# Layer-0 attention: 512-column evictions of the probabilities, V's two parts multiplied onto the same rows for later queries, and output casts on GpSimd

## The chip, the cores and the metric

The kernel runs on one core of a Trainium2 chip. The metric is the device time of one execution in microseconds (us), the median of several runs. Five engines matter: TensorE (PE; its weight loads are shown as PEld), VectorE (DVE), ScalarE (ACT), GpSimd (POOL) and SyncE (SP), which issues most DMAs. Each works through its own queue in order, and waits on semaphores for the others.

## The reference

The model is a trunk of four layers over 512 latent tokens and 256 context tokens, width 1024. Each layer has a mixer (grouped attention, neighbourhood attention, a convolution module, a Fourier mixer) and a squared-ReLU MLP. Only the mixer of layer 0 concerns the change: attention with 16 query heads, 4 key and value heads, and a head width of 64. Latent queries look at all 768 keys, context queries at the 256 context keys alone.

```
def gqa_attend(q, k, v):
    s = jnp.einsum('bqkgd,bnkd->bkgqn', q, k, preferred_element_type=jnp.float32)
    p = jax.nn.softmax(s, axis=-1).astype(v.dtype)
    return jnp.einsum('bkgqn,bnkd->bqkgd', p, v)
...
k_all = jnp.concatenate([kc, kl], axis=1)
yl = gqa_attend(q_latent, k_all, v_all) @ w_o      # in blocks of 128 queries
yc = gqa_attend(q_context, kc, vc) @ w_o
```

Everything is float32. The kernel's matmuls take operands of type float32r, and it splits a float32 operand in two such parts: H, the value cast to float32r, and L, what is left (the value minus H). A product of two split operands is then H*H + H*L + L*H, and sometimes L*L as well.

## The kernel before, in words

The stage of the change is `l0b`. It works on 8 pairs of heads. Each pair has three parts of 256 queries: part 0 (latent queries 0 to 255), part 1 (latent queries 256 to 511) and part 2 (the context queries). Parts 0 and 1 have 6 chunks of 128 keys, part 2 has 2. A work item is one head (`hh`) of one part of one pair, 48 in all. For each item `front` is called twice, for `u` = 0 and 1, 128 queries each, and `back` is called twice, one item behind: its first half stands between the two fronts of the next item, its second half after them.

`front` multiplies the scores on PE into a PSUM tile `s` (L612; two such tiles), takes the negated maximum of each row on DVE (L614), and the exponential with the row's sum on ACT (L616). It then transposes the probabilities on PE, three chunks of 128 x 128 to one PSUM tile `st` (L621; three such tiles), and evicts each of these tiles with `split` (L104, L105): ACT casts it to the tile H of the transposed probabilities (`pt[0]`), and DVE subtracts to get L (`pt[1]`). In part 2 a front has only two chunks.

`back` multiplies V by these probabilities (L635). `vp` holds for each key chunk and each key head 128 columns, 64 of V's H and then 64 of V's L, so one matmul with 128 weight columns gives H's product in PSUM rows 0 to 63 and L's in rows 64 to 127. It is done once with `pt[0]` and once with `pt[1]`; 256 columns (both query halves) stream through. There is one PSUM tile `pv`; the two heads of a pair take 256 columns each. When the second head is complete, `recip_rows` makes the reciprocals of the sums (DVE, L555), spreads each over 64 columns (DVE, L557), transposes that on PE (L559) and copies it out on ACT (L561) as `rb`. `fold` adds PSUM rows 64 to 127 to rows 0 to 63, or the other way round for the second head: an ACT copy (L567) and a DVE add (L568) for each head. `scale_pv` multiplies by `rb` on POOL (L573), casts to H on ACT (L104) and subtracts for L on POOL (L105).

A planner inside the framework sets the order of instructions on each engine, from the order in which the program issues them and from its own estimate of durations; the order is then fixed. Instructions that are issued earlier go first where both are ready. Two instructions on different engines that touch one PSUM tile follow each other.

Towards the end of the stage the first weights of the output projection are loaded and split (ACT casts, POOL or DVE subtracts, 1024 columns each). The projection starts on PE as soon as the attention's last matmuls are issued, and takes the eight pairs' outputs in order, the context queries in its second half. `recip_rows` is also called by layer 1's attention.

Of the kernel before, what the change touches and what calls it, by code (L numbers as in the profile page):

```python
# [9 lines left out]
F = mybir.dt.float32  # L10
R = mybir.dt.float32r
BF = mybir.dt.bfloat16
AF = mybir.ActivationFunctionType
ALU = mybir.AluOpType
AX = mybir.AxisListType

P = 128
# [7 lines left out]
HD = 64  # L25
# [24 lines left out]
class Trunk:  # L50
# [496 lines left out]
                            nc.tensor.transpose(pt[:, i * P:(i + 1) * P], pf[s][:, t, 2 * hp + hh].rearrange("p s d -> p (s d)"), self.ident)  # L547
                    nc.scalar.copy(out=self.kd[:, 2 * hp:2 * hp + 2, s, c0:c0 + 256], in_=pt.rearrange("p (h t) -> p h t", h=2))

    def recip_rows(self, sums, w, wk, rp):  # L550

        nc = self.nc
        nb = w // P
        rs = wk.tile([P, nb, 2], F, tag="rs", name="rs", bufs=3)
        nc.vector.reciprocal(out=rs, in_=sums)  # L555
        re = self.tmp("q", w)
        nc.vector.tensor_copy(out=re.rearrange("p (b h d) -> p b h d", b=nb, h=2), in_=rs.unsqueeze(3).to_broadcast([P, nb, 2, HD]))  # L557
        for b in range(nb):
            nc.tensor.transpose(rp[:, b * P:(b + 1) * P], re[:, b * P:(b + 1) * P], self.ident)  # L559
        rb = self.tmp("r", w)  # L560
        nc.scalar.copy(out=rb, in_=rp[:, :w])  # L561
        return rb
# [13 lines left out]
    def l0b(self):  # L576
        nc, io = self.nc, self.io
        self.psum("psum4", s=(2, 2))
        op = self.open("o0", "right")
        o = [op.tile([P, 2, TALL], R, name=f"o0_{j}") for j in range(KC)]  # L580
        wk = self.open("att0", "right")
        qs, groups, heads, pvs = {}, {}, {}, {}

        def load(pair):
            qs[pair] = self.kv.tile([P, 2, TALL], R, tag="q", name="q", bufs=2)
# [3 lines left out]
        def keys(part):  # L589
            return (0, 6) if part < 2 else (4, 2)  # L590

        def alloc(pair, part, hh):
            n = len(heads)
            pool, bufs = (self.pools["att0b"], 1) if n % 3 == 2 and "att0b" in self.pools else (wk, 2)
            heads[pair, part, hh] = [pool.tile([P, 2, 6, P], R, tag=f"pt{s}", name=f"pt{s}", bufs=bufs)[:, :, :keys(part)[1]] for s in range(2)]

        def front(pair, part, hh, u):

            k0, nk = keys(part)
            if hh == u == 0:  # L600
                groups[pair, part] = wk.tile([P, 2, 2], F, tag="sums", name="sums", bufs=3)
            if u == 0 and (pair, part, hh) not in heads:
                alloc(pair, part, hh)
            q, sums, pt = qs[pair], groups[pair, part], heads[pair, part, hh]
            ps = self.ps("s")
            t0 = part * 256 + u * P
            kc = k0 * P
            for c0, c1 in ((0, 512), (512, TALL)):
                if c1 <= kc:
                    continue  # L610
                for s in range(2):
                    nc.tensor.matmul(ps[:, c0:c1], q[:, hh, t0:t0 + P], self.kd[:, pair // 2, s, c0:c1], start=(s == 0), stop=(s == 1))  # L612
            mx = self.small(1, "m")
            nc.vector.tensor_reduce(out=mx, in_=ps[:, kc:TALL], axis=AX.X, op=ALU.max, negate=True)  # L614
            p = wk.tile([P, TALL], F, tag="p", name="p", bufs=3)
            nc.scalar.activation(p[:, kc:], ps[:, kc:TALL], AF.Exp, bias=mx, accum_out=sums[:, u, hh:hh + 1])  # L616
            for c in range(k0, 6, 3):
                n = min(3, 6 - c)
                pp = self.ps("st")
                for i in range(n):  # L620
                    nc.tensor.transpose(pp[:, i * P:(i + 1) * P], p[:, (c + i) * P:(c + i + 1) * P], self.ident)  # L621
                pw = pp[:, :n * P].rearrange("p (c q) -> p c q", c=n)
                self.split(pw, pt[0][:, u, c - k0:c - k0 + n], pt[1][:, u, c - k0:c - k0 + n])

        def back(pair, part, hh, half):

            k0, nk = keys(part)
            if hh == half == 0:
                pvs[pair, part] = self.ps("pv")
            sums, pv = groups[pair, part], pvs[pair, part]  # L630
            pt = heads[pair, part, hh]
            o_ = pv[:, hh * 256:hh * 256 + 256]
            for c in range(k0 + half * nk // 2, k0 + (half + 1) * nk // 2):
                for s in range(2):
                    nc.tensor.matmul(o_, self.vp[:, c, pair // 2].rearrange("p s d -> p (s d)"), pt[s][:, :, c - k0],  # L635
                                     start=(hh == s == 0 and c == k0), stop=(hh == s == 1 and c == 5))
            if hh == half == 1:
                t0 = part * 256
                rb = self.recip_rows(sums, 256, wk, self.ps("st"))
                t = self.tmp("t", 256)  # L640
                for e in range(2):
                    self.fold(pv[:, e * 256:e * 256 + 256], e, t)
                self.scale_pv(t, rb, (o[pair][:, 0, t0:t0 + 256], o[pair][:, 1, t0:t0 + 256]))

        work = [(pair, part, hh) for pair in range(8) for part in range(3) for hh in range(2)]
        alloc(0, 0, 0)
        load(0)
        for i in range(len(work) + 1):
# [709 lines left out]
```

## Time and profile before

| | |
|---|---|
| median of 3 runs | 2746.52 us (2746.07 to 2748.45) |
| profiled execution | 2748.76 us, its span 2747.0 us |
| granted clock of PE, mean | 0.985 of 2.4 GHz |
| PE busy | 2638.0 us, 96% of the span |
| DVE busy | 1776.1 us, 65% |
| ACT busy | 1154.8 us, 42% |
| POOL busy | 405.4 us, 15% |

The span is the time from the first to the last instruction of the profiled execution; its own time is a little longer. A busy time counts each moment in which at least one instruction of the engine was under way. A matmul's end is modelled in the profile, and neighbouring matmuls overlap, so the mean duration of a matmul is longer than its share of PE's time. The attention stage of layer 0 lies between about 181 and 388 us of the span.

### The profile page before, as it was taken

To read this page: it belongs to the slowest core of one execution; us is meant where nothing else is said; L and a number is where in the kernel's file an instruction comes from. 1 tells how busy PE (TensorE), PEld (TensorE's weight loads), DVE (VectorE), ACT (ScalarE), POOL (GpSimd) and SP (SyncE) were. 2 spreads that over 40 slices of the span, in tenths; PEclk is the share of its full clock that TensorE was granted. 3 is DMA by queue.
4 is the path that set the end of the run, shared out by engine and by line. 5 is a ranking of instruction groups with operands and counts; after the bars stand their busy time and mean duration, and the time that the engine had idled before them with its cause. 6 is when DMAs were issued, how large, how long until landed. Compare 5 with 4: busy or idle time off the path is not lost.

```text
span 2747.0 us, 39895 instructions
## 1 busy us (share of the span) xinstructions
PE 2638.0 (96%) x15472; PEld 2316.5 (84%) x15472; DVE 1776.1 (65%) x2827; ACT 1154.8 (42%) x2052; POOL 405.4 (15%) x359
## 2 busy tenths in 40 slices
PE   7989899999999999998999999998999998999998
PEld 5878778888888888988988889888888887988888
DVE  7988879766453372268766657998666657644445
ACT  3458864212121342268523335656322245533323
POOL 2321212000000030034200004543000012200002
PEclk8999999999999999999999999999999999999999
DMA  7431234445442256488466644213466633333334
GB/s 269 133 123 36 77 120 147 139 145 153 137 140 85 77 168 209 138 201 190 161 206 207 190 147 139 77 47 107 133 212 200 206 124 107 123 115 94 98 100 123
DMA packets 124844, 384.85 MB, mean 140 GB/s; under 512 B 17264, under 2 KB 37872, under 8 KB 123632
## 3 DMA queue, kind: packets, MB, share of 16 engines
q1 hardware_dynamic: 121392, 379.17, 44.2%
q10 hardware_dynamic: 3264, 3.15, 0.3%
q8 instruction: 122, 2.00, 0.3%
q14 instruction: 66, 0.54, 0.1%
HBM read 354.98 MB, written 27.26 MB: 139 GB/s over the span
## 4 chain that ended last, share of the span: by engine, by line
PE 49%; DVE 4%; DMA 2%; ACT 1%; issue 0%; POOL 0%; DVEq 0%; SPq 0%; ACTq 0%; POOLq 0%
PE ps_mm L124 15%; PE ps_mm L125 15%; PE ps_mm L127 15%; DVE ps_st L1162 1%; DMA k<-k 1%; DMA q<-q 1%; PE ps_cv L124 1%; PE ps_cv L125 1%; PE ps_cv L127 1%; DVE h L182 0%; PE ps_s L881 0%; PE ps_pt L890 0%; PE ps_cv L995 0%; PE ps_cv L998 0%; PE ps_cv L999 0%
## 5 line engine op out<-in xcount | busy, mean ns | idle before, releaser
L104 ACT CAST wh<-raw 128x1024 fp32r<-128x1024 f32 (+1 forms) x397 | 419.6, 1060 | 1030.6 <-PE ps_mm L125 606.5
L105 DVE TENSOR_TENSOR wl<-raw,wh 128x1024 fp32r<-128x1024 f32 (+1 forms) x368 | 463.7, 1262 | 372.6 <-ACT wh L104 369.5
L194 POOL TENSOR_TENSOR S<-S,tmp_q 128x256 f32<-128x256 f32 (+1 forms) x104 | 144.8, 1392 | 1684.8 <-ACT tmp_q L193 1680.7
L124 PE MATMUL ps_mm<-u,wh 128*128 128x512 f32 (+1 forms) x1088 | 374.9, 346 | 0.0
L125 PE MATMUL ps_mm<-u,wh 128*128 128x512 f32 (+1 forms) x1088 | 373.8, 345 | 0.0
L127 PE MATMUL ps_mm<-u,wl 128*128 128x512 f32 (+1 forms) x1088 | 373.6, 346 | 0.0
L125 PE MATMUL ps_mm<-hm,wh 128*128 128x512 f32 (+1 forms) x912 | 331.2, 365 | 0.0
L127 PE MATMUL ps_mm<-hm,wl 128*128 128x512 f32 (+1 forms) x912 | 331.0, 365 | 0.0
L124 PE MATMUL ps_mm<-hm,wh 128*128 128x512 f32 (+1 forms) x912 | 328.2, 366 | 1.1 <-ACT hm L181 1.1
L223 DVE CUSTOM_DVE_ANT_0 prod<-araw,sb 128x1024 bf16<-128x1024 f32 x224 | 276.4, 1234 | 6.5 <-DMA araw<-in_ada 5.3
L206 DVE SCALAR_TENSOR_TENSOR x<-ps_mm,mod,x 128x256 f32<-128x256 f32 (+1 forms) x192 | 115.1, 605 | 246.8 <-PE ps_mm L127 241.1
L125 PEld LDWEIGHTS ps_mm<-u,wh 128*128 128x128 f32 x1088 | 206.1, 189 | 25.0
L127 PEld LDWEIGHTS ps_mm<-u,wl 128*128 128x128 f32 x1088 | 205.9, 189 | 25.2
L124 PEld LDWEIGHTS ps_mm<-u,wh 128*128 128x128 f32 x1088 | 205.7, 189 | 25.3 <-DVE x L206 0.4
L127 PEld LDWEIGHTS ps_mm<-hm,wl 128*128 128x128 f32 x912 | 172.6, 189 | 27.6 <-DVE wl L105 0.4
L125 PEld LDWEIGHTS ps_mm<-hm,wh 128*128 128x128 f32 x912 | 172.7, 190 | 27.2
L124 PEld LDWEIGHTS ps_mm<-hm,wh 128*128 128x128 f32 x912 | 170.8, 190 | 28.7 <-ACT hm L181 1.5
L104 ACT CAST u<-tmp_r 128x512 fp32r<-128x512 f32 (+2 forms) x143 | 89.0, 624 | 171.1 <-DVE tmp_r L738 170.9
L124 PE MATMUL ps_big<-hm,wh 128*128 128x512 f32 x464 | 157.4, 339 | 0.8 <-ACT wh L104 0.8
L105 DVE TENSOR_TENSOR u<-tmp_r,u 128x512 fp32r<-128x512 f32 (+2 forms) x143 | 99.1, 695 | 86.6 <-ACT u L104 86.2
L125 PE MATMUL ps_big<-hm,wh 128*128 128x512 f32 x464 | 145.9, 337 | 0.0
L124 PE MATMUL ps_mm<-wh,h 128*128 128x256 f32 x448 | 129.9, 291 | 7.3 <-DVE tmp_r L499 2.9
(311 smaller groups left out, 5781.6 us busy)
## 6 DMA issues: line engine op xcount, KB each, us to landing
raw<-in_w SPq DMA_DIRECT2D x288, 512.0 KB, 3.9
araw<-in_ada SPq DMA_DIRECT2D x176, 512.0 KB, 3.7
raw<-in_wo SPq DMA_DIRECT2D x32, 512.0 KB, 4.3
raw<-in_wpw SPq DMA_DIRECT2D x24, 512.0 KB, 3.5
raw<-in_wqk SPq DMA_DIRECT2D x16, 512.0 KB, 4.1
q<-q SPq DMA_DIRECT2D x32, 256.0 KB, 9.1
raw<-in_wft SPq DMA_DIRECT2D x16, 512.0 KB, 3.8
k<-k SPq DMA_DIRECT2D x32, 224.0 KB, 9.4
```

The source lines that it names most:

```text
L104: self.nc.scalar.copy(out=H, in_=src)
L105: (low or self.nc.vector).tensor_tensor(out=L, in0=src, in1=H.bitcast(F), op=ALU.subtract)
L124: mm(o, lhs[0], rh, start=(k == 0), stop=False)
L125: mm(o, lhs[0], rl, start=False, stop=False)
L127: mm(o, lhs[1], rh, start=False, stop=last)
L194: (add or nc.gpsimd).tensor_tensor(out=S[:, :w], in0=S[:, :w], in1=q, op=ALU.add)
L206: self.nc.vector.scalar_tensor_tensor(out=xm, in0=self.like(ps), scalar=gate[:, m:m + 1], in1=xm, op0=ALU.mult, op1=ALU.add)
L223: ins = self.nc.vector.tensor_tensor_reduce(out=junk, in0=t, in1=self.sb[:, v], op0=ALU.mult, op1=ALU.add, scale=1.0, scalar=0.0, accum_ou ...
L1162: keep(nc.vector.scalar_tensor_tensor(out=y if last else a, in0=ut, scalar=wt, in1=a, op0=ALU.mult, op1=ALU.add))
```

## The change

Three things are changed, all in `l0b` and the helper `recip_rows`. The transposed probabilities of one head are now taken four chunks to a PSUM tile, running on from the first 128 queries to the second, so that each eviction has 512 columns; `pt` is one flat tile of the same size. In parts 1 and 2, `back` multiplies V's H by both parts of the probabilities and V's L by their H, three matmuls with 64 weight columns each, all onto PSUM rows 0 to 63 (V's L times the probabilities' L is left out there), and DVE multiplies the sum by `rb` straight out of PSUM. Part 0 keeps its two matmuls, its folds and its multiplication on POOL. In all parts POOL casts the output to H, and POOL spreads the reciprocals.

```diff
-    def recip_rows(self, sums, w, wk, rp):
+    def recip_rows(self, sums, w, wk, rp, spread=None):
...
-        nc.vector.tensor_copy(out=re.rearrange("p (b h d) -> p b h d", b=nb, h=2), in_=rs.unsqueeze(3).to_broadcast([P, nb, 2, HD]))
+        (spread or nc.vector).tensor_copy(out=re.rearrange("p (b h d) -> p b h d", b=nb, h=2), in_=rs.unsqueeze(3).to_broadcast([P, nb, 2, HD]))
...
-            for c in range(k0, 6, 3):
-                n = min(3, 6 - c)
-                pp = self.ps("st")
-                for i in range(n):
-                    nc.tensor.transpose(pp[:, i * P:(i + 1) * P], p[:, (c + i) * P:(c + i + 1) * P], self.ident)
-                pw = pp[:, :n * P].rearrange("p (c q) -> p c q", c=n)
-                self.split(pw, pt[0][:, u, c - k0:c - k0 + n], pt[1][:, u, c - k0:c - k0 + n])
+            for c in range(k0, 6):
+                i = u * nk + c - k0
+                if i % 4 == 0:
+                    turned[0] = self.ps("st")
+                pp = turned[0]
+                nc.tensor.transpose(pp[:, i % 4 * P:i % 4 * P + P], p[:, c * P:c * P + P], self.ident)
+                if i % 4 == 3:
+                    self.split(pp, *(t[:, (i - 3) * P:(i + 1) * P] for t in pt))
...
-            for c in range(k0 + half * nk // 2, k0 + (half + 1) * nk // 2):
-                for s in range(2):
-                    nc.tensor.matmul(o_, self.vp[:, c, pair // 2].rearrange("p s d -> p (s d)"), pt[s][:, :, c - k0],
-                                     start=(hh == s == 0 and c == k0), stop=(hh == s == 1 and c == 5))
+            for c in range(half * nk // 2, (half + 1) * nk // 2):
+                flags = hh == c == 0, hh == 1 and c == nk - 1
+                if part == 0:
+                    v = self.vp[:, k0 + c, pair // 2].rearrange("p s d -> p (s d)")
+                    for s in range(2):
+                        nc.tensor.matmul(pv[:, cols], v, pt[s][:, :, c], start=flags[0] and s == 0, stop=flags[1] and s == 1)
+                else:
+                    for i, (v, s) in enumerate(((0, 0), (0, 1), (1, 0))):
+                        nc.tensor.matmul(pv[:HD, cols], self.vp[:, k0 + c, pair // 2, v], pt[s][:, :, c], start=flags[0] and i == 0, stop=flags[1] and i == 2)
             if hh == half == 1:
                 t0 = part * 256
-                rb = self.recip_rows(sums, 256, wk, self.ps("st"))
+                rb = self.recip_rows(sums, 256, wk, self.ps("st"), nc.gpsimd)
                 t = self.tmp("t", 256)
                 for e in range(2):
-                    self.fold(pv[:, e * 256:e * 256 + 256], e, t)
-                self.scale_pv(t, rb, (o[pair][:, 0, t0:t0 + 256], o[pair][:, 1, t0:t0 + 256]))
+                    a, pe = slice(e * HD, e * HD + HD), pv[:, e * 256:e * 256 + 256]
+                    if part == 0:
+                        self.fold(pe, e, t)
+                    else:
+                        nc.vector.tensor_tensor(out=t[a], in0=pe[:HD], in1=rb[a], op=ALU.mult)
+                if part == 0:
+                    nc.gpsimd.tensor_tensor(out=t, in0=t, in1=rb, op=ALU.mult)
+                H, L = (o[pair][:, s, t0:t0 + 256] for s in range(2))
+                nc.gpsimd.tensor_copy(out=H, in_=t)
+                nc.gpsimd.tensor_tensor(out=L, in0=t, in1=H.bitcast(F), op=ALU.subtract)
```

## Rows read from the trace of the kernel before

**Rows 1.** The page's list of engines: busy us, share of the span, instructions.
```profile
PE 2638.0 (96%) x15472; PEld 2316.5 (84%) x15472; DVE 1776.1 (65%) x2827; ACT 1154.8 (42%) x2052; POOL 405.4 (15%) x359
```

**Rows 2.** Busy times by stretch (length, engines, PEclk, DMA, GB/s): one pair, weights stretch.
```profile
276.12:299.78 23.66, 21.82 (x159) 19.35 (x160) 21.39 (x45) 21.07 (x57) 4.42 (x7) 1.00 0.11 34
...
323.42:353.87 30.45, 25.96 (x169) 22.88 (x169) 25.27 (x52) 25.79 (x66) 9.05 (x8) 0.89 0.38 130
```

**Rows 3.** Groups by shape, four pairs (228.81 to 323.42 us): busy, mean ns, idle before.
```profile
L621 PE MATMUL ps_st<-ident,p 128*128 128x128 f32 x224 | 36.9, 277 | 5.7 <-ACT p L616 3.0 <-ACT tmp_r L561 2.4
L635 PE MATMUL ps_pv<-pt,vp 128*128 128x256 f32 x224 | 35.9, 291 | 0.3
L105 DVE TENSOR_TENSOR pt<-ps_st,pt 128x384 fp32r<-128x384 f32 x65 | 34.7, 550 | 2.7 <-ACT pt L104 1.9
L104 ACT CAST pt<-ps_st 128x384 fp32r<-128x384 f32 x65 | 30.4, 489 | 4.8 <-PE ps_st L621 4.6
...
L568 DVE TENSOR_TENSOR tmp_t<-ps_pv,tmp_t 64x256 f32<-64x256 f32 x24 | 10.1, 420 | 4.1 <-ACT tmp_t L567 3.4
...
L573 POOL TENSOR_TENSOR tmp_t<-tmp_t,tmp_r 128x256 f32<-128x256 f32 x12 | 8.9, 741 | 65.3 <-DVE tmp_t L568 49.8 <-ACT pt L104 15.5
...
L567 ACT COPY tmp_t<-ps_pv 64x256 f32<-64x256 f32 x24 | 8.8, 367 | 4.7 <-PE ps_pv L635 4.2
...
L105 DVE TENSOR_TENSOR pt<-ps_st,pt 128x256 fp32r<-128x256 f32 x16 | 6.4, 420 | 0.1
L104 ACT CAST pt<-ps_st 128x256 fp32r<-128x256 f32 x16 | 5.6, 375 | 0.3
L104 ACT CAST o<-tmp_t 128x256 fp32r<-128x256 f32 x12 | 5.4, 447 | 0.0
...
L557 DVE COPY tmp_q<-rs 128x256 f32<-128x256 f32 x12 | 3.5, 288 | 0.1
```

**Rows 4.** Timeline of PE in one pair (start, length, neighbours of a kind merged).
```profile
285.37 0.49 PE L621 MATMUL ps_st<-ident,p 128*128 128x128 f32 x3
...
291.63 1.58 PE L635 MATMUL ps_pv<-pt,vp 128*128 128x256 f32 x12
```

**Rows 5.** Waits of PE's weight loads, same four pairs: us in total, times, longest.
```profile
PEld ps_st L621 <- ACT p L616: 4.9, 8, 0.6
PEld ps_st L621 <- ACT tmp_r L561: 4.2, 8, 0.9
PEld ps_s L612 <- ACT p L616: 3.6, 9, 0.6
```

**Rows 6.** Like operations elsewhere: layer 1's groups, single lines (min/median/max ns).
```profile
L105 DVE TENSOR_TENSOR pt<-ps_pt,pt 128x512 fp32r<-128x512 f32 x49 | 32.3, 679 | 1.2 <-ACT pt L104 1.1
...
L104 ACT CAST pt<-ps_pt 128x512 fp32r<-128x512 f32 x49 | 27.8, 589 | 6.0 <-PE ps_pt L890 5.9
...
L969 POOL COPY S<-y x1: 612/612/612, 1749.8 to 1749.8; 128x512 f32<-128x512 f32 x1
...
L124 PE MATMUL ps_mm<-u,wh x1088: 277/389/504, 932.2 to 2735.6; 128*128 128x512 f32 x107, 128*128 128x256 f32 x75
...
L124 PE MATMUL ps_st<-d,ny x4: 397/513/774, 2299.2 to 2321.2; 128*4 128x512 f32 x4
```

**Rows 7.** Timeline of ACT and DVE at the ends of parts 1 and 2.
```profile
282.36 0.37 ACT L561 COPY tmp_r<-ps_st 128x256 f32<-128x256 f32 x1
...
284.05 0.43 DVE L568 TENSOR_TENSOR tmp_t<-ps_pv,tmp_t 64x256 f32<-64x256 f32 x1 [0.21 <-ACT tmp_t L567]
...
289.23 0.37 ACT L561 COPY tmp_r<-ps_st 128x256 f32<-128x256 f32 x1
...
290.38 0.43 DVE L568 TENSOR_TENSOR tmp_t<-ps_pv,tmp_t 64x256 f32<-64x256 f32 x1
```

**Rows 8.** Timeline of POOL in the stretch in which it prepares weights.
```profile
334.29 2.35 POOL L105 TENSOR_TENSOR wl<-raw,wh 128x1024 fp32r<-128x1024 f32 x1 [1.68 <-ACT wh L104]
```

**Rows 9.** Timeline of PE at the stage's end.
```profile
383.33 1.22 PE L635 MATMUL ps_pv<-pt,vp 128*128 128x256 f32 x8 [1.08 <-DVE tmp_t L568]
```

More of the change, by code (lines that the diff above doesn't have):

```diff
@@ L581, in l0b @@
         wk = self.open("att0", "right")
-        qs, groups, heads, pvs = {}, {}, {}, {}
+        qs, groups, heads, pvs, turned = {}, {}, {}, {}, [None]
         def load(pair):
@@ L594, in alloc @@
             pool, bufs = (self.pools["att0b"], 1) if n % 3 == 2 and "att0b" in self.pools else (wk, 2)
-            heads[pair, part, hh] = [pool.tile([P, 2, 6, P], R, tag=f"pt{s}", name=f"pt{s}", bufs=bufs)[:, :, :keys(part)[1]] for s in range(2)]
+            heads[pair, part, hh] = [pool.tile([P, 12 * P], R, tag=f"pt{s}", name=f"pt{s}", bufs=bufs)[:, :2 * P * keys(part)[1]] for s in range(2)]
         def front(pair, part, hh, u):
@@ L630, in back @@
             sums, pv = groups[pair, part], pvs[pair, part]
-            pt = heads[pair, part, hh]
-            o_ = pv[:, hh * 256:hh * 256 + 256]
-            for c in range(k0 + half * nk // 2, k0 + (half + 1) * nk // 2):
-                for s in range(2):
-                    nc.tensor.matmul(o_, self.vp[:, c, pair // 2].rearrange("p s d -> p (s d)"), pt[s][:, :, c - k0],
-                                     start=(hh == s == 0 and c == k0), stop=(hh == s == 1 and c == 5))
+            pt = [t.rearrange("p (u c q) -> p u c q", u=2, c=nk) for t in heads[pair, part, hh]]
@@ new lines, in back @@
+            cols = slice(hh * 256, hh * 256 + 256)
+            for c in range(half * nk // 2, (half + 1) * nk // 2):
[7 more added lines that the diff above has]
+                        nc.tensor.matmul(pv[:HD, cols], self.vp[:, k0 + c, pair // 2, v], pt[s][:, :, c], start=flags[0] and i == 0, stop=flags[1] and i == 2)
```

## The prediction

> **What bounds the kernel now.** I read the page first: PE is busy 96% of the span, so time saved beside PE is worth only what PE waits for [rows 1]. The change touches one stage, the attention of layer 0 (about 181 to 388 us), so next come the busy times of its stretches. One pair of heads takes 23.65 us, the same four times over, and PE, DVE and ACT are each busy 21.0 to 21.8 us of it: nothing has room. The next stretch, where the output weights are prepared as well, takes 30.45 us at a mean granted clock of 0.89 [rows 2].
>
> Third, the groups by shape over exactly four pairs give the price of each instruction [rows 3]. PE I count by distance between starts. Twelve probability-value (PV) matmuls take 1.58 us and one alone 0.29, so the next comes after (1.58-0.29)/11 = 0.117 us [rows 3, 4]. Three transposes take 0.49 us and one alone 0.277: 0.107 us [rows 3, 4]. Per pair: 62 transposes (56 of probabilities, 6 of reciprocals) 6.6 us; 56 PV and 24 score matmuls of 256 columns, 9.4 us; 16 score matmuls of 512 columns at twice 0.117 (an estimate), 3.7 us. Together 19.7 us, so 23.65-19.7 = 3.9 us of waits. The waits say whose: PE's weight loads, which go ahead of its matmuls, waited 4.9+4.2+3.6 = 12.7 us in four pairs for ACT: for an exponential to transpose, for a PSUM tile behind the reciprocal copy, for a score tile that an exponential still reads [rows 5]. That is 3.2 of the 3.9 us of a pair.
>
> Busy time and distances disagree on PE: by busy time 23.65-21.8 = 1.85 us is free in a pair, by distances 3.9 [rows 2]. The Trainium skill (Trainium Kernel Development and Optimization, Performance Expectations) says that busy matmul time is a poor measure because matmuls are pipelined, and that the busy share of weight loads is a good one. That share is 19.35 us of the pair [rows 2], near my 19.7: the trace agrees. By plain busy time the added matmuls below (1.87 us) would use up all of PE's room and the sum would be no gain; by the weight loads there is room for twice that.
>
> **The change part by part, per pair.**
>
> *Evictions of 512 columns.* Today a pair has 16 of 384 columns and 4 of 256; afterwards 14 of 512, the same elements. ACT: 16 x 0.489 + 4 x 0.375 = 9.3 us against 14 x 0.589 (the 512-column eviction of layer 1) = 8.2: -1.1 us. DVE: 16 x 0.550 + 4 x 0.420 = 10.5 against 14 x 0.679 = 9.5: -1.0 us [rows 3, 6]. Price: of the six transposes of the first 128 queries two now sit in a half-filled PSUM tile until those of the second 128 join them, so one of three such tiles is held through the PV half that is issued between. Turnover falls from 4 tiles to 3 per head, which about balances it, and the longest wait behind a tile is 0.9 us today [rows 5]. For context queries all four transposes share one tile; PV needs both query halves of a tile anyway, so it waits no longer. I take 0, bounds -0.9 to +0.9 us a pair, one such wait less or more.
>
> *Three 64-row matmuls for two 128-row ones, parts 1 and 2.* Per head 6 more in part 1 and 2 more in part 2: 16 a pair, all on PE, all in a row with other PV work. No row has 64 columns of weights. With 4 columns a matmul that streams 512 takes 0.397 us at best, no less than the median of those with 128, 0.389 [rows 6]: the streamed columns set it. I take 0.117 each: 16 x 0.117 = +1.87 us. Bounds: not below 0.107 (a transpose's distance, half the columns), up to 0.29 (nothing pipelined), 1.7 to 4.6 us.
>
> *Folds.* In parts 1 and 2 the four ACT copies go, 4 x 0.367 = -1.5 us of ACT; DVE's adds become multiplications of the same shape with one operand in PSUM, 0.42 each: 0 [rows 3]. POOL's multiplication goes from two groups of three. Today the one PV tile comes free only after copy, add, copy, add, which take turns: part 1's last add ends at 284.48 and part 2's at 290.81 [rows 7], and PV of the next pair starts right behind, at 291.63 [rows 4]. Afterwards two adjacent DVE instructions free it, once the reciprocal rows are there.
>
> *The added wait.* The multiplication needs those rows, which come by DVE reciprocal, POOL spread, two PE transposes, ACT copy. The sums are complete one head earlier, so the start can run ahead; but the transposes and the ACT copy are issued after this head's fronts. In part 1 the copy ended at 282.73 (282.36+0.37), well before the last add; in part 2 at 289.60, 1.2 us before today's release [rows 7]. So release moves from 284.48 to about 283.6 (282.73 and two of 0.42) and from 290.81 to about 290.4: 0.4 to 0.9 us earlier, not later. If the rows came late, the next evictions and maxima would stand behind the multiplication on DVE, then ACT's exponentials, then PE. I count no gain of its own for the release; it is how PE's waits can shrink.
>
> *Spread and casts on POOL.* DVE loses 3 x 0.288 = 0.9 us, ACT 3 x 0.447 = 1.3 us [rows 3]. POOL gets three spreads and three casts of 256 columns and loses two multiplications of 0.741. A POOL copy of 512 columns took 0.612 us, a two-input instruction of 256 0.741 [rows 3, 6]; I take 0.4 each (between half the first and the second, nearer the like operation), bounds 0.3 to 0.74. POOL: 4.4 [rows 2] + 6 x 0.4 - 1.5 = 5.3 us of 23.65, cover enough. If the cover is gone, as where POOL prepares weights for 2.35 us twice, a spread stands behind that, up to 2.4 us once or twice in the kernel [rows 8].
>
> **The sum.** Per pair ACT loses 1.1+1.5+1.3 = 3.9 of 21.0 busy us and DVE 1.0+0.9 = 1.9 of 21.4 (a little less where neighbours overlap by a tenth of a us), and PE goes from 19.7 to 21.6. PE becomes the bound. Ends for the pair: 21.6 us if PE never waits, 25.5 if all 3.9 us stay. Between, I take a little over three fifths of the waits gone (ACT, which ends 3.2 of 3.9, is 18% lighter, and PV frees its tile sooner): 21.6+1.4 = 23.0, or -0.65; eight pairs: -5.2 us. The long stretch lost 30.45-23.65 = 6.8 us to weight casts on ACT and POOL and the clock; the lighter ACT may give back 0 to 3.4, taken -1.0. At the end PE waited 1.08 us for a fold's add [rows 9]: -0.5. Behind the stage, PE goes on with projections at once and its loads are issued at the stage's end, so the saving carries through. Together -6.7 us: the profiled execution's 2748.76 us (span 2747.0 and 1.8 around it) becomes 2742.1. It lies 2.2 us above the median of the runs, 2746.52, so as a median: **2739.8 us**. A difference of under 0.2%, 5.5 us, is no change here: below 2741.0 counts as faster, above 2752.0 as slower.
>
> **Rivals.**
>
> *PE takes back what ACT gives.* Only the waits equal to the added 1.87 us go: a pair stays at 23.65 within 0.4, the edges give 0 to -1.5: 2743 to 2750, middle 2746. For it: the three engines are balanced, the order is fixed in advance and each engine takes its queue in order, so relief on one reaches PE only in part. Against: 3.2 of 3.9 us of the waits name ACT, and ACT is relieved by more than that.
>
> *PE as the bound, its waits unchanged (slower).* Place: the chain score, maximum, exponential, transpose within one head, whose instructions the change leaves as they are. If PE's waits for exponentials (4.9 of 12.7 us) and score tiles (3.6) are the latency of that chain and not ACT's load, two thirds of all waits stay, and if the copy behind the third stays where it is in the queue, that too, and the 128 added matmuls come on top: 8 x 1.87 = +15, 2761.5 us. It decides from where fewer than 1.2 us of waits a pair go. For it: those two kinds of wait are 8.5 of 12.7 us [rows 5]. Against: the wait behind the reciprocal copy, 4.2 us, is a place in ACT's queue, and the fold's copies leave that queue.
>
> *PE nearly dense.* Nearly all waits go and the long stretch gives half back: 8 x -2.05 - 3.4 = -20, 2727 us; midway 2731. For it: without ACT's 3.9 us PE can run ahead by two score tiles. Against: no stretch of this stage has PE so dense.
>
> **How the numbers follow.** Forecast (2736 to 2743) 0.42, PE nearly dense 0.14, no change 0.24, slower 0.20. Faster by over 0.2%: the dense case and six sevenths of the forecast's range, 0.50; within it 0.32 (no change, the rest of the forecast, a little of the slower case); slower 0.18. The slower case runs from 2751 (1.2 us of waits gone a pair) to 2761.5, the dense one from 2727 to 2735. The range leaves out about half of each: 2729 to 2756, and 0.17 of the chance; the matmul's upper bound (4.6 us a pair) lies beyond it and has its chance in what is left out.
>
> **What would show it.** 112 evictions of 512 columns at about 0.59 (ACT) and 0.68 us (DVE); in parts 1 and 2 PV matmuls 0.117 us apart with shorter weight loads; a pair of 22.5 to 23.3 us with PE's weight loads busy about 21 of it; waits of PE on ACT at half or less; spreads near 0.4 us on POOL. Wrong, if the 64-row matmuls stand clearly more than 0.117 us apart, if DVE waits for the reciprocal rows more than 0.3 us a group, or if transposes wait for a half-filled tile.

## The result and the profile after

The changed kernel takes 2763.22 us (median of 4 runs, 2760.67 to 2765.56), the kernel before beside it on the same chip 2747.48: ratio 1.0057 [1.0041, 1.0072], 0.57% slower. The forecast was 2739.8 us, range 2729 to 2756: the time lies outside it and on the other side of no change.

The page's list of engines of the changed kernel, to be read against [rows 1]:

```profile
PE 2650.8 (96%) x15600; PEld 2335.1 (85%) x15600; DVE 1766.1 (64%) x2755; ACT 1135.7 (41%) x1948; POOL 410.8 (15%) x391
```

128 matmuls more, 19 us less of ACT and 10 us less of DVE, and a longer time. The busy times of four steady pairs of the attention stage (start and end, length, busy time and count by engine, granted clock, DMA share, GB/s):

```profile
222.72:323.60 100.88, 92.33 (x698) 84.01 (x697) 81.71 (x142) 74.48 (x173) 20.95 (x40) 1.00 0.10 32
```

A pair takes 100.88/4 = 25.22 us, before 23.65 [rows 2]. ACT is now busy 18.6 us of it and DVE 20.4, before 21.0 and 21.4. Every price that was forecast for a single instruction is there, in the groups by shape of the same stretch (busy us, mean ns | idle before):

```profile
L105 DVE TENSOR_TENSOR pt<-ps_st,pt 128x512 fp32r<-128x512 f32 x57 | 38.1, 684 | 7.9 <-ACT pt L104 7.5
...
L104 ACT CAST pt<-ps_st 128x512 fp32r<-128x512 f32 x57 | 32.2, 589 | 15.3 <-PE ps_st L622 14.9
...
L616 ACT ACTIVATE p<-ps_s,small_m 128x768 f32<-128x768 f32 x32 | 29.0, 906 | 8.3 <-DVE small_m L614 8.2
...
L643 PE MATMUL ps_pv<-pt,vp 128*64 128x256 f32 x192 | 25.8, 279 | 2.3 <-DVE tmp_t L568 1.8
...
L643 PEld LDWEIGHTS ps_pv<-pt,vp 128*64 128x64 f32 x192 | 22.2, 134 | 3.8 <-DVE tmp_t L568 2.3 <-DVE pt L105 1.5
...
L640 PEld LDWEIGHTS ps_pv<-pt,vp 128*128 128x128 f32 x97 | 12.2, 188 | 0.1
...
L653 DVE TENSOR_TENSOR tmp_t<-ps_pv,tmp_r 64x256 f32<-64x256 f32 x16 | 6.6, 415 | 1.0 <-PE ps_pv L643 0.8
...
L657 POOL CAST o<-tmp_t 128x256 fp32r<-128x256 f32 x12 | 4.8, 401 | 30.1 <-DVE tmp_t L653 30.1
L557 POOL COPY tmp_q<-rs 128x256 f32<-128x256 f32 x12 | 4.8, 399 | 18.2 <-DVE rs L555 17.9
```

The reader is to look at the idle column. Before, ACT's evictions of 384 columns stood idle for 4.8 us in four pairs, nearly all of it for PE [rows 3]; now those of 512 stand for 15.3. The exponentials (L616) now stand for 8.3 us, for DVE's maxima; before, the same 32 stood for 0.1:

```profile
L616 ACT ACTIVATE p<-ps_s,small_m 128x768 f32<-128x768 f32 x32 | 29.2, 912 | 0.1
```

The relieved engines stand and wait for PE and for each other. PE in its turn waits for them as before: the waits of its weight loads (us in total, times, longest), to be read against [rows 5]:

```profile
PEld ps_st L622 <- ACT p L616: 5.4, 10, 0.9
PEld ps_st L622 <- ACT tmp_r L561: 2.6, 2, 1.3
PEld ps_pv L643 <- DVE tmp_t L568: 2.3, 2, 1.1
PEld ps_pv L643 <- DVE pt L105: 1.5, 4, 0.4
PEld ps_st L559 <- issue: 1.1, 2, 0.6
PEld ps_s L612 <- ACT p L616: 0.7, 2, 0.4
```

The whole list makes 13.6 us. Before, the three kinds of [rows 5] made 12.7, and two smaller ones stood beside them, which brings that list to 14.9:

```profile
PEld ps_pv L635 <- DVE pt L105: 1.1, 4, 0.3
PEld ps_st L621 <- PE ps_s L612: 1.1, 4, 0.3
```

The wait for score tiles nearly went (3.6 to 0.7) and the one behind the reciprocal copy fell (4.2 to 2.6), but PV now waits 3.8 us for a fold and for evictions where it waited 1.1, and the wait for exponentials is no shorter. The 64-row matmuls stand where the forecast put them, PE's timeline (start, length):

```profile
287.03 1.45 PE L643 MATMUL ps_pv<-pt,vp 128*64 128x256 f32 x11
```

(1.45-0.28)/10 = 0.117 us apart. At the stage's end, against [rows 9]:

```profile
395.71 1.62 PE L643 MATMUL ps_pv<-pt,vp 128*64 128x256 f32 x12 [0.38 <-DVE tmp_t L653]
397.17 0.40 PE L124 MATMUL ps_mm<-o,wh 128*128 128x512 f32 x1
```

The wait there fell from 1.08 to 0.38 us. But the output projection starts at 397.2 us of the span, before at 384.4: 12.8 us later. The two profiled executions differ by 11.9 us in their spans (2758.9 and 2747.0), so in them the stage holds all of the loss; the medians differ by 15.7. By parts: the start and first pair +2.8, the four steady pairs +6.3, the sixth pair +2.0, the seventh +2.7, the end -1.0.

### The profile page after: what moved, and what is told of

It reads as the page before. It is cut to its first block, busy times and chain, and to the rows that moved or that the text cites. A ratio compares the mean times of both kernels' runs of the same rounds, so it can differ in the third digit from the quotient of the medians.

```text
span 2758.9 us, 40112 instructions
## 1 busy us (share of the span) xinstructions
PE 2650.8 (96%) x15600; PEld 2335.1 (85%) x15600; DVE 1766.1 (64%) x2755; ACT 1135.7 (41%) x1948; POOL 410.8 (15%) x391
## 4 chain that ended last, share of the span: by engine, by line
PE 50%; DVE 3%; DMA 1%; ACT 1%; issue 0%; POOL 0%; DVEq 0%; ACTq 0%; SPq 0%
PE ps_mm L124 15%; PE ps_mm L125 15%; PE ps_mm L127 15%; DMA k<-k 1%; PE ps_cv L124 1%; PE ps_cv L125 1%; PE ps_cv L127 1%; DVE ps_st L1177 1%; DVE h L182 0%; DMA q<-q 0%; PE ps_s L896 0%; DVE pt L105 0%; PE ps_pt L905 0%; DVE wl L105 0%; ACT p L902 0%
```

## The experiments

A is the eviction of 512 columns, B the 64-row matmuls with DVE's multiplication, C the spread and the casts on POOL. "Pair" is the mean of four steady pairs (the first reciprocal of a pair to that of the fourth after it, a quarter), "end" the start of the first projection matmul in the span. Ratios are against the kernel before.

| kernel | pair, us | end, us | ratio |
|---|---|---|---|
| before | 23.65 | 384.4 | 1 |
| changed (A, B, C) | 25.22 | 397.2 | 1.0057 [1.0041, 1.0072] |
| e1: A, C | 24.53 | 389.2 | 1.0029 [1.0018, 1.0040] |
| e2: B, C | 24.79 | 393.1 | 1.0055 [1.0037, 1.0073] |
| e3: A, B | 25.50 | 397.7 | 1.0055 [1.0038, 1.0072] |
| e4: changed, two 64-row matmuls of three | 24.83 | 389.0 | 1.0023 [1.0014, 1.0032] |
| e5: A | 24.89 | 391.3 | 1.0025 [1.0013, 1.0036] |
| e6: B | 24.63 | 390.8 | 1.0020 [1.0010, 1.0029] |
| e7: C | 23.18 | 383.1 | 1.0010 [0.9998, 1.0022] |
| e8: before, 4 + 2 chunks to an eviction | 24.12 | 388.6 | 1.0019 [1.0009, 1.0028] |
| e9: A, PE's sequence of before | 25.53 | 398.3 | 1.0056 [1.0039, 1.0073] |
| e10: A, last transposes issued late | 24.89 | 391.4 | 1.0028 [1.0017, 1.0039] |
| e11: B, PE's sequence of before | 24.72 | 394.1 | 1.0044 [1.0029, 1.0059] |
| e12: A, B, C, PE's sequence of before | 25.58 | 398.6 | 1.0073 [1.0057, 1.0090] |
| e13: A, no tile held | 24.91 | 391.7 | 1.0031 [1.0021, 1.0042] |
| e14: C, PE's sequence of before | 24.65 | 389.2 | 1.0019 [1.0010, 1.0028] |
| e15: casts on POOL, all sequences of before | 23.41 | 385.7 | 1.0003 [0.9994, 1.0013] |
| e16: C, all sequences of before | 23.41 | 384.8 | 1.0016 [1.0006, 1.0025] |
| e17: B, all sequences of before | 25.72 | 399.8 | 1.0058 [1.0043, 1.0073] |
| e18: B and casts, all sequences of before | 25.73 | 400.3 | 1.0050 [1.0035, 1.0065] |

The ends explain the totals to within -2 to +6 us. What is left over comes behind the stage, in code that no edit touches, or from one execution to the next (the ends are those of one profiled execution each; e7's took 2758.91 us with the earliest end of all). It is not explained by these runs, so small steps are read from the pairs. Pairs can alternate: e6's take 26.3, 22.8, 26.5 and 22.8 us, and only their mean is used.

### Each part undone, and each alone

**e1, B undone** (three places):

```diff
-                if part == 0:
+                if part < 3:
```

> The changed kernel with parts 1 and 2 computed as part 0 is: two matmuls with 128 weight columns, folds on ACT and DVE, the multiplication on POOL; evictions of 512 columns, POOL's spreads and casts stay. Theory 1 (PE is the bound; the 128 added matmuls come on top of waits that stay): the whole loss goes with them, 2740 to 2748 us, 15 us under the changed kernel's 2763; PE's waits per pair as before, 3 to 4 us. Theory 2 (the PSUM tile held half-filled from one set of queries to the next, and coarser evictions, delay the PV matmuls): little comes back, 2756 to 2763. Theory 3 (the planner's new order is poor, whatever was changed): between, with pairs of unequal length.

**e2, A undone**; this front stands in e6 and e7 too:

```diff
-            for c in range(k0, 6):
-                i = u * nk + c - k0
...
+            for c in range(k0, 6, 3):
+                n = min(3, 6 - c)
...
+                pp = self.ps("st")
...
```

> The changed kernel with the evictions as before (three chunks to a tile, within one set of 128 queries); the 64-row matmuls and POOL's spreads and casts stay. Theory 1: no gain, 2763 to 2768 us, since ACT and DVE only lose what was saved in evictions and PE keeps its 128 added matmuls. Theory 2: 2745 to 2755, the waits of ACT for a full tile (14.9 us in four pairs) fall back to 5. Theory 3: anywhere, pairs of another length pattern than 26.2 and 24.2 us in turn.

**e3, C undone**:

```diff
-                rb = self.recip_rows(sums, 256, wk, self.ps("st"), nc.gpsimd)
+                rb = self.recip_rows(sums, 256, wk, self.ps("st"))
...
-                nc.gpsimd.tensor_copy(out=H, in_=t)
+                nc.scalar.copy(out=H, in_=t)
```

> The changed kernel with the spreads back on DVE and the output casts back on ACT; evictions of 512 and the 64-row matmuls stay. Theory 1: 2763 to 2768 us, ACT and DVE have room for 1.3 and 0.9 us a pair. Theory 2: the same. A theory 4 (the reciprocal rows come late because POOL's queue delays the spread, and so the PV tile): 2750 to 2757.

**e4, V's low part left out in parts 1 and 2**:

```diff
-                    for i, (v, s) in enumerate(((0, 0), (0, 1), (1, 0))):
+                    for i, (v, s) in enumerate(((0, 0), (0, 1))):
```

> The changed kernel without the third 64-row matmul of each chunk in parts 1 and 2 (the product of V's low part is left out there), so that PE has as many matmuls as before the change, while everything else of it stays. Theory 1: all of the loss goes and more, 2738 to 2750 us. Theories 2 and 4: 2755 to 2763, since the matmuls were hidden and the waits stay. Theory 3: between.

No single part is the culprit: with any one undone the kernel is still slower than before. e4 has everything of the change but the 128 added matmuls, and its end lies at 389.0, where e1 lies, which has the folds back, and its pairs are 0.30 us longer than e1's: no gain from the folds' relief shows beside A, each in its own sequence. By the end, the 128 matmuls cost 397.2-389.0 = 8.2 us of the 15.0 that they take on PE; by the steady pairs 0.39 of 1.87.

**e5, e6, e7: A, B and C alone** (the edits of e1 and e3; e2 and e3; e1 and e2).

> The kernel before with one part of the change alone: evictions of 512 columns that run on from the first 128 queries to the second. Matmuls, folds, spreads and casts as before. Theory 2 (a tile held half-filled delays what follows): slower than before by 6 to 10 us, 2754 to 2759, though ACT and DVE have 1.1 and 1.0 us less to do in a pair; more waits of ACT's casts for transposes and of PE for exponentials. Theory 1 (only PE's matmuls count): 2740 to 2749.

> The kernel before with the 64-row matmuls and the multiplication on DVE in parts 1 and 2 alone; evictions, spreads and casts as before. Theory 1 (PE as the bound, its waits unchanged): 2758 to 2765 us. Theory 2: the matmuls cost what taking them out of the changed kernel gave back, 5 to 8 us: 2753 to 2757.

> The kernel before with the spreads and the output casts on POOL alone; matmuls, folds and evictions as before. Theories 1 and 2: no change or a little faster, 2741 to 2750 us. Theory 4 (reciprocal rows late through POOL): 2752 to 2757.

Alone the parts cost a pair +1.24, +0.98 and -0.47 us, in sum +1.75 where the whole change costs 1.57. But two by two they don't add: B with C takes 24.79 us where 24.16 would follow, and undoing A in the changed kernel gives 0.43 and not 1.24. So a part's price depends on what else is there, by up to 0.8 us a pair. Sure is that A alone, with no more work than before and 2.1 us less by the rows of its evictions, costs 1.24 us in the sequence that the planner makes for it. What PE waits for in e5's four pairs (221.81 to 321.38):

```profile
PE ps_pv L640 <- DVE tmp_t L568: 4.2, 4, 1.0
PE ps_s L612 <- ACT p L616: 2.6, 4, 0.7
PE ps_st L622 <- ACT p L616: 1.9, 5, 0.4
PE ps_st L622 <- ACT tmp_r L561: 1.5, 4, 0.4
```

PV stands before the one PV tile that the folds still hold; that wait is not among those of before [rows 5].

**e8, uneven evictions within one front** (against the kernel before): the same ACT and DVE work to 2% (0.589+0.375 against twice 0.489), no tile shared by two fronts.

```diff
-            for c in range(k0, 6, 3):
-                n = min(3, 6 - c)
+            for c in range(k0, 6, 4):
+                n = min(4, 6 - c)
```

> The kernel before with its evictions cut as 512 and 256 columns within each set of 128 queries, instead of 384 and 384: as many evictions as before, none across two sets, all else as before. Theory 2 in its narrow form (the holding across two sets is what costs): 2744 to 2752 us. Theory 2 in its wide form (a wider eviction by itself starts later and stops the next transposes, whatever is held): 2752 to 2757. Theory 3 (any other split of the work makes the planner find a poorer order): slower as well, with pairs of unequal length or other waits than those for exponentials.

A pair costs 0.47 us more though nothing is held across fronts and no work is added. So evictions cut in another way can cost time without a held tile. The planner ordered ACT and DVE anew here too, so the run doesn't say whether the widths or the order did it.

### Is it the planner's new sequence, or the held tile?

In e9, e11, e12 and e14 PE's instructions of the stage are tied by issue-order edges to the sequence that the kernel before has; in e11 and e12 the second PV matmul of a chunk stands for two in parts 1 and 2.

```diff
+        for kind, n in re.findall(r"([stvR])([0-9]+)", ORDER0):
+            for _ in range(int(n)):
+                ins = marks[kind].pop(0)
+                if last is not None:
+                    self.tc.add_manual_dep(ins, last.name, mybir.DependencyInfo(mybir.DependencyClass.NoSync, mybir.DependencyReason.DATA), reason="order")
+                last = ins
```

> The 512-column evictions alone, with PE's scores, transposes, PV and reciprocal transposes of the stage tied into exactly the sequence that the kernel before has on PE (by issue-order edges; nothing waits longer for data). The same edits with the planner's own sequence reached the first projection matmul at 391.3 us (before: 384.4). Theory planner: the 7 us come from the new sequence that the planner chose from its estimates; then this run is at 381 to 386 us and the total at 2743 to 2749. Theory hold and width: a half-filled tile and later evictions delay PE whatever the sequence; then 389 us or more, total 2752 to 2760, and PE waits for evictions at tiles that used to be ready.

> The 64-row PV matmuls and DVE's multiplication alone, with PE's sequence of the kernel before (each second matmul of a key chunk in parts 1 and 2 replaced by two). With the planner's own sequence the first projection matmul came at 390.8. Theory PE bound: 128 matmuls of 0.117 are on PE's path and the sequence matters little, 389 to 395 us, total 2752 to 2760. Theory planner: the sequence was a part of the cost, 386 us or less.

> The whole change with PE's sequence of the kernel before (second PV matmuls of a chunk doubled in parts 1 and 2). With the planner's own sequence: first projection matmul at 397.2, total 2763. Theory planner: the new sequence is what costs, 384 to 390 us and a total of 2746 to 2754. Theory PE bound with hold and width: 394 to 402 us, total 2758 to 2768.

Giving PE its old sequence back doesn't help: all three are slower in it than in the planner's. But ACT and DVE were not tied, and the planner ordered them anew (line numbers are shifted in kernels with added code: here scores are L641, transposes L651, PV L669, DVE's eviction L117). e9 allows a comparison place by place, since PE, though not ACT and DVE, does the same things in the same order. The same PV run of e9 and, under it, of the kernel before (PE's timeline; start, length, idle before):

```profile
277.11 0.37 PE L669 MATMUL ps_pv<-pt,vp 128*128 128x256 f32 x1
277.31 0.49 PE L651 MATMUL ps_st<-ident,p 128*128 128x128 f32 x3
277.56 0.70 PE L669 MATMUL ps_pv<-pt,vp 128*128 128x256 f32 x4
278.67 1.10 PE L669 MATMUL ps_pv<-pt,vp 128*128 128x256 f32 x7 [0.41 <-DVE pt L117]
```

```profile
270.68 0.37 PE L635 MATMUL ps_pv<-pt,vp 128*128 128x256 f32 x1
270.88 0.49 PE L621 MATMUL ps_st<-ident,p 128*128 128x128 f32 x3
271.13 1.55 PE L635 MATMUL ps_pv<-pt,vp 128*128 128x256 f32 x11
```

After five matmuls of this head, the sixth waits in e9 for DVE: chunk 2 with the low part. Chunks 2 to 5 of the second 128 queries share one 512-column tile; before, chunk 2 stood in the third of four tiles and the fourth held chunks 3 to 5 alone. So PV's first half now needs the head's last eviction. That is one part of the cause at this place; the other is DVE's order, in e9 and, under it, before:

```profile
277.06 0.96 DVE L643 TENSOR_REDUCE small_m<-ps_s 128x1 f32<-128x768 f32 x1 [0.70 <-PE ps_s L641]
277.94 1.28 DVE L117 TENSOR_TENSOR pt<-ps_st,pt 128x512 fp32r<-128x512 f32 x2
```

```profile
270.44 0.56 DVE L105 TENSOR_TENSOR pt<-ps_st,pt 128x384 fp32r<-128x384 f32 x1 [0.48 <-ACT pt L104]
270.91 0.95 DVE L614 TENSOR_REDUCE small_m<-ps_s 128x1 f32<-128x768 f32 x1
```

Before, DVE evicts the head's last tile first and then takes the next front's maximum; in e9 the maximum goes ahead. ACT's cast of the tile ended at 277.33 (276.75 and 0.58 long), so the eviction of 0.68 us could have ended at 278.01, and the sixth matmul, due at 278.11, would hardly have waited (the maximum would then have come later). PV waits so eight times in four pairs, at two places of each pair. At the other place (0.50 to 0.52 us) two shorter maxima stand ahead, the eviction begins 0.22 us after its cast has ended, and about 0.3 us of the wait would remain without them. The three longest waits of e9's four pairs (222.72 to 324.85), against [rows 5]:

```profile
PEld ps_s L641 <- ACT p L645: 6.8, 8, 1.5
PEld ps_st L651 <- ACT p L645: 6.1, 8, 0.8
PEld ps_pv L669 <- DVE pt L117: 5.3, 8, 0.7
```

Waits for exponentials grew from 8.5 to 12.9 us and PV's wait for evictions from 1.1 to 5.3, while the 4.2 us behind the reciprocal copy are no longer in the list: what the change took from one wait it gave to two others. How A's price divides between the wider evictions and the new order of ACT and DVE is not shown; no run has A with all three engines tied.

**e10, e13: A without the hold.** In e10 the last two transposes of the first queries are issued with those of the second:

```diff
+            late = [(p, c) for c in range(k0, 6)]
+            if u == 0:
+                n = nk // 4 * 4
+                late, turned[0] = late[:n], late[n:]
...
```

> The 512-column evictions alone, but the last two transposes of the first 128 queries are issued with those of the second 128 (context queries: all four together), so that no PSUM tile is half-filled while a PV half is issued. Theory hold: the cost of the 512-column evictions (+7.0 us at the first projection matmul, 391.3) goes, 383 to 386 us and a total of 2743 to 2749. Theory width (later evictions of larger tiles) and theory planner: it stays within 388 to 393 us, total 2752 to 2758.

It tests nothing: the planner put these transposes where they had been, and the pairs are the same. In e13 PE's sequence itself is tied: the planner's of e5, with four transposes of a tile in a row at the place of the last.

```diff
-R2 t4 s2 t2 v12 t6 s2
+R2 t4 s2 v12 t8 s2
```

(a stretch of the sequence: R are the reciprocal's transposes, t the others, s scores, v PV, each with its count; the two transposes that stood ahead of v12 now stand behind it)

> The 512-column evictions alone, in the sequence that the planner chose for them on PE, except that from the fourth pair's start (third pair in part) to the seventh pair the four transposes of a tile stand in a row at the place of the last one, so that no tile is held half-filled across other work of PE (one of the fourteen tiles of a pair, of the context queries, stays as it was). The planner's sequence had pairs of 25.0 us and the first projection matmul at 391.3. Theory hold: pairs fall to 24.0 us or less. Theory lateness of larger tiles (PE waits for whole evictions and for exponentials behind them, whether a tile is held or not): pairs stay at 24.7 us or more, and the first projection matmul at 390 or later.

Three pairs with the tied rows (the first of them in part) take 75.19 us (244.68 to 319.87) and in e5 75.14: doing away with the held tile gives nothing back. PE's waits in them:

```profile
PE ps_pv L669 <- DVE tmp_t L584: 7.5, 9, 1.0
PE ps_s L641 <- ACT p L645: 0.9, 3, 0.3
PE ps_st L651 <- ACT p L645: 0.6, 3, 0.2
```

Here too PE waits for other things in the place of those that went: for the folds 2.5 us a pair, in e5 1.05. The theory of the hold falls; that larger tiles come late stands, beside the planner's order on ACT and DVE, which no run with A holds. What wasn't tried either is a 512-column eviction that keeps chunk 2 out of the last tile.

### What relief is worth

**e14, C with PE's sequence of before** (the edges shown above).

> Spread and output cast on POOL alone, with PE's sequence of the kernel before: pure relief (ACT -1.3, DVE -0.9 us of busy time a pair), no work of PE added and no sequence changed. With the planner's own sequence pairs went from 23.65 to 23.2 us. Theory relief turns into PE time (the forecast's three fifths of the waits): pairs of 22.6 us or less, total 2739 to 2745. Theory relief reaches PE only in part: pairs of 23.0 to 23.6, first projection matmul 380 to 384, total 2743 to 2749. A late reciprocal row (POOL behind its weight work) would show as pairs above 23.65.

A surprise: less work on ACT and DVE, PE's sequence untouched, and a pair of 24.65 us. ACT and DVE were still sequenced anew. So e15 to e18 tie all three engines, the sequences taken from the kernel before, less what leaves an engine:

```diff
+        self.in_order(ON_PE, ON_ACT, ON_DVE)
```

> Only the output casts move from ACT to POOL; scores, transposes, PV, maxima, exponentials, evictions, folds and reciprocal rows of the stage keep the kernel before's sequence on PE, ACT and DVE. Pure relief of ACT, 1.3 us a pair, off the path of any matmul. Theory relief turns into PE time by the forecast's three fifths: pairs of 22.9 us or less. Theory relief of an engine that PE doesn't wait for at that place is worth little: pairs of 23.4 to 23.7. No theory has a pair above 23.8; if one is, the estimate that a fixed sequence with less work can't be slower is wrong.

> Casts and spreads both on POOL, sequences on PE, ACT and DVE fixed as before. The run with only PE's sequence fixed had pairs of 24.65 us. Theory ACT's and DVE's new sequences did that: pairs of 23.7 us or less here. Theory the spread on POOL comes late for its place in PE's sequence: pairs of 24.2 us or more, and the reciprocal's transposes wait for POOL.

Both take 23.41 us: the spread on POOL isn't late, and e14's loss was ACT's and DVE's new sequence. In an unchanged sequence 1.3 us less of ACT by the rows (0.87 by its busy time) give a pair 0.24 us, and 0.9 us less of DVE give nothing. PE's waits in e15's four pairs (222.46 to 316.11):

```profile
PEld ps_st L667 <- ACT tmp_r L592: 6.3, 8, 0.8
PEld ps_st L667 <- ACT p L661: 3.8, 8, 0.7
PEld ps_s L657 <- ACT p L661: 2.2, 8, 0.3
PEld ps_pv L686 <- DVE pt L670: 1.1, 4, 0.3
```

Two of the three kinds of [rows 5] got shorter and the one behind the reciprocal copy longer (4.2 to 6.3).

> The 64-row PV matmuls and DVE's multiplication alone, sequences on PE, ACT and DVE fixed as before (folds of parts 1 and 2 left out of ACT's, multiplications in the places of the adds on DVE). Theory PE bound with its waits unchanged: 23.65 + 1.87 = 25.5 us a pair, first projection matmul near 399. Theory waits shrink by the folds' relief: 24.3 to 25.0 (the planner's own sequence gave 24.6 and 390.8 us). Forecast's theory: 23.0 to 23.7.

> The same with the output casts on POOL as well (ACT -1.5 and -1.3 us a pair). Theory relief turns into PE time: at least 0.5 us a pair less than the run without the casts moved. Theory what PE still waits for is the chain score, maximum, exponential and not ACT's load: within 0.2 us of it.

By the sum the added matmuls come wholly on top: 25.72-23.65 = 2.07 us against 1.87 of work, end +15.4, and the casts' relief gives nothing (25.73). But PE's old waits did not stay. Its weight loads in e17's four pairs (223.87 to 326.73):

```profile
PEld ps_st L667 <- DVE pt L670: 6.2, 4, 1.5
PEld ps_st L667 <- ACT tmp_r L592: 3.2, 4, 0.8
PEld ps_st L667 <- ACT p L661: 3.1, 8, 0.5
PEld ps_s L657 <- ACT p L661: 1.0, 4, 0.3
```

The three kinds of [rows 5] fell from 12.7 to 7.3 us, and a new one, once a pair, took 6.2. Where it comes from is seen in the timeline (POOL and weight loads left out):

```profile
296.96 0.38 ACT L592 COPY tmp_r<-ps_st 128x256 f32<-128x256 f32 x1
...
297.44 0.42 DVE L699 TENSOR_TENSOR tmp_t<-ps_pv,tmp_r 64x256 f32<-64x256 f32 x1 [1.73 <-ACT tmp_r L592]
297.79 0.94 DVE L659 TENSOR_REDUCE small_m<-ps_s 128x1 f32<-128x768 f32 x1
298.65 1.00 DVE L670 TENSOR_TENSOR pt<-ps_st,pt 128x384 fp32r<-128x384 f32 x2
298.82 0.90 ACT L661 ACTIVATE p<-ps_s,small_m 128x768 f32<-128x768 f32 x1 [1.48 <-DVE small_m L659]
...
299.24 1.17 PE L667 MATMUL ps_st<-ident,p 128*128 128x128 f32 x6 [1.30 <-DVE pt L670]
```

In the add's old place the multiplication waits 1.73 us for the reciprocal rows; behind it on DVE stand a maximum and two evictions, and PE loses 1.30 us. So e17 holds three things at once, the matmuls, shorter old waits and this new one; that they add up to about the matmuls' work is chance. In the planner's own sequences the multiplications stand later: in the changed kernel they wait 0.25 us a pair (L653 above). With PE's sequence alone held (e11) the same matmuls cost 1.07 us a pair. No run gave a version faster than before: C alone has the shortest pairs, but its total isn't below.

## Why the prediction was wrong, point by point

**Prices of instructions: right.** 0.117 us for a 64-row matmul, 0.589 and 0.684 for the evictions, 0.40 on POOL, 0.415 for the multiplication: each within 0.01 of the forecast.

**The relief of ACT and DVE: over-sized.** Forecast -3.9 and -1.9 us a pair, measured 21.0-18.6 = -2.4 and -1.0. Neighbouring instructions overlap: e15 takes three casts of 0.447 us off ACT and its busy time falls from 84.21 to 80.72 us in four pairs, 0.87 a pair and not 1.34.

**Evictions, "I take 0, bounds -0.9 to +0.9": outside the bounds alone, inside them in the whole change.** Alone they cost +1.24 us a pair, +1.88 in PE's old sequence, and in the changed kernel 0.43 (against e2). The price that the prediction weighed, the held tile, is nothing (e13). That PV "waits no longer" it said of the context queries only. For the latent ones it left out that PV's first half comes to need the last tile (e9), and it left out everywhere that the planner orders ACT and DVE anew; e9 shows both in one wait, and no run divides the cost between them. The Trainium skill (Perfetto Trace Analysis, Optimizing Scalar/DVE Operations) says that larger operations can raise throughput if the engine is saturated. The rows agree on throughput (14 evictions take 1.1 us less of ACT by their rows), but the time rose: in e9's list PE waits for single exponentials and evictions.

**"A little over three fifths of the waits gone": the step that decides.** It asked for 2.5 of 3.9 us a pair, and so for a pair of 23.0. Measured: a pair of 25.22, and 25.22-19.7-1.87 = 3.65 left, 0.3 gone. By parts (pair less PE's work): B 3.06, so 0.9 gone with it; C 3.5, 0.5 gone; A 5.2, 1.2 added. In fixed sequences 1.3 us of relief shortens the waits by 0.24 (e15) and by nothing in e18, where the new wait behind the multiplication is the longest (6.2 us in four pairs, as in e17). The prediction took the engine named as the last releaser for an engine that lacks time, and relief of it for time that PE gets. What the runs showed in its place: PE's waits moved rather than went (14.9 us in the list before, 13.6 after, for a fold and evictions where they had been for score tiles and the reciprocal copy), and the relieved ACT stood idle for PE and DVE. That it had been waiting for PE before as well, a little earlier in the same ring of score, maximum, exponential, transpose, eviction and PV, fits these rows but is not shown by itself. A second thing left out is the order: the edits made the planner order ACT and DVE anew, which alone can cost a pair 1.24 us (e14 against e16). How much of the miss in the changed kernel is order stays open. None of the three signs of being wrong that the prediction named came up; the waits went to places that it hadn't named.

**The weight loads' share.** It was right as a measure of PE's work (84.01 of 100.88 us here against 77.27 of 94.61 before, 83 and 82%). A part of the room was used, since the added 1.87 us cost a steady pair 0.39 (e4) to 0.98 us (e6). The waits beyond that, on which the forecast counted, did not go.

**The added wait: right for the planner's sequence, and the reason is now known.** In the changed kernel the multiplications stand idle 1.0 us in four pairs, 0.8 of it for PE. In the adds' places it would be 9.6 us, DVE's waits in e17's four pairs (223.87 to 326.73):

```profile
DVE tmp_t L699 <- ACT tmp_r L592: 9.6, 8, 1.7
DVE small_m L659 <- PE ps_s L657: 4.3, 4, 1.1
```

**The edges: failed with the pairs.** The end gave its 0.7 us (-0.5 forecast), but the sixth and seventh pair, forecast -0.65 each and -1.0 for the long stretch, cost 4.7, and the start with the first pair 2.8. No run explains these singly.

**The rivals.** The slower one named 2761.5 us, 1.7 from the median, and its point of decision held: fewer than 1.2 us of waits went. Its make-up was only partly true, so that its total came so near is in part luck: it has 1.87 us for each of eight pairs, the steady ones cost 1.57, and the medians hold 2.9 us that the stage doesn't. Nor did the waits stay as they were; even where B costs its whole work (e17), the old ones got shorter and a new one took their place. In the changed kernel B costs 0.69 (against e1) to 0.98 us (alone), and the evictions, which the rival left at nothing, 0.43 (against e2) to 1.24.

## What to carry to other kernels

Where three engines hand each other results in a ring, and each is near 90% busy, don't count relief of one as time of the bound engine because it is named as the last releaser. Here 2.2 us less by the rows gave a pair 0.47 us in one sequence (e7), 0.24 in another (e16) and a loss of 1.00 in a third (e14). Added work of the bound engine cost between a fifth of itself (e4) and a little more than all of it (e17, where a new wait came with it); the waits around it decided. Before merging evictions, list which chunks the next reader needs first, which instruction now delivers the last of them, and what stands ahead of that instruction in its engine's queue. A kernel whose sequence a planner fixes should be compared with the sequence held too, on every engine: here the sequence of ACT and DVE alone moved a pair by 1.24 us (e14 against e16), as much as the edits did, and holding PE's alone (e9) proved little.

## What the runs showed of the hardware

A weight load of 64 columns took 134 ns against 188 for 128, but 256 streamed columns kept the matmuls 0.117 us apart in both. POOL needed 0.40 us for a copy or cast of 128 x 256 (399 and 401 ns). Two of the PV runs shown took about 0.1 us more than these distances give: seven matmuls behind e9's stall 1.10 us, where 0.28+6 x 0.117 = 0.98 would be expected, and eleven behind transposes in the kernel before, with no wait ahead of them, 1.55 where 0.28+10 x 0.117 = 1.45 would. What the 0.1 us is, no run shows.
